# Three retention output units in seven-product form, with their operand's sums stored earlier, and a new order of the input projection

## The chip, the core and the metric

The kernel runs on one core of a Trainium2 chip. The core has a matrix engine (PE, with a separate row PEld for its weight loads), a vector engine (DVE), a scalar engine (ACT), a general engine (POOL) and a queue engine (SP). Each engine takes its instructions strictly in the order in which they were built, and waits on semaphores of the others. In this kernel SP issues nearly all transfers between HBM and on-chip memory; POOL issues a few.

The metric is the device time of one execution in microseconds (us). Smaller is better.

## What is computed

One layer of a gated hybrid encoder on 1024 positions with 1024 channels, all in float32. Cut to what matters here:

```python
h = rms_norm(x, norm1_w)
q, k, v, g_ret, x_lru, y_lru, gate_ret, gate_lru = split(h @ w_in)
o = head_group_norm(chunkwise_retention(rotary(q), rotary(k), v), ret_gn_w)
y_a = (o * silu(g_ret)) @ w_ret_o              # retention output
hl = rg_lru(causal_depthwise_conv(x_lru))
y_b = (hl * gelu(y_lru)) @ w_lru_o             # recurrent output
mix = sigmoid(gate_ret + b0) * y_a + sigmoid(gate_lru + b1) * y_b
x = x + mix @ w_out
x = x + (gelu(conv(h2 @ w_up_gate)) * (h2 @ w_up_val)) @ w_dn,  h2 = rms_norm(x)
return rms_norm(x)
```

## The kernel before

**Precision.** A float32 operand is split into two fast-format parts, `hi` (an ACT copy, line 167) and `lo` (a DVE subtraction, line 168), in the function `split`. A float32 product is three matrix instructions: hi·hi, hi·lo and lo·hi (`PASSES`).

**Units.** All large products are cut into units of 256 output channels, 1024 input channels and 1024 positions, a 2×2 by 2×2 block product. A unit has one of two forms.

- The standard form (`mm_std`, line 329): eight block products, each 4 column tiles × 3 passes = 12 matrix instructions of 128×512, so 96 in all. Its weights need four splits, and its results go from PSUM straight to the unit's own last step.
- The seven-product form (`mm_fast`, line 359, Strassen's scheme as Winograd arranged it): seven block products, 84 matrix instructions. Its weights need four sums (lines 245, 248, 254, 261) and seven splits. Three of its intermediate results are copied out of PSUM by ACT (line 374) and added by DVE (line 385). It also needs four sums of the moving operand, `T1` to `T4`, besides the four blocks `B11` to `B22`. Each of these names stands for four tiles of 128×512.

**Stages.** The stages follow each other on PE: the input projection (28 units), retention output (4 units, `w_ro`), recurrent output (4 units, `w_lo`), the output projection (line 1009), the up projection (24 units), and the down projection (12 units). The first two stages and the third form one list of jobs, `jobs`; the order of the input projection is written by hand in the string `SEQ`. A letter `g` is a merge-gate unit, `y` a gelu branch unit, `x` a recurrent branch unit followed by its recurrent block (`lru_block`), `h0` to `h3` are the three units of a retention head followed by its attention work (`rotary_head`, `retention_head`, `ret_out`). Before, `SEQ` ends in `... y3 x3`, so the last unit is a recurrent one and its block runs beside the retention output.

**Side work.** What follows a unit is a Python generator, and it is dealt out in small steps between the block products: `advance` for the recurrent and retention work, `build` for the splits of the next stage's operand (`operand`, `tsets`), as long as at least 20 of the `NU` = 78 buffers of 128×512 are free. `need` forces a split out when a product wants it. A scheduler then orders the instructions of each engine by these priorities.

**Retention output.** `ret_out` multiplies the normalised head by its gate and stores the result in HBM as `og_d` (line 837). When the last but one unit of the projection is done, `og_start` appends a builder that reads `og_d` back (line 867) and splits the 16 tiles of `B11` to `B22`. All four units have standard form (`FAST_RO = 0`), so no `T` sums are made. The three last recurrent output units have seven-product form (`FAST_LO = 3`); their operand `u` is read from `u_d` at line 867 too. `u_start` starts that builder when the third retention output unit is done, after draining the recurrent blocks.

Of the kernel before, what the change touches and what calls it, by code (L numbers as in the profile page):

```python
# [11 lines left out]
F32 = mybir.dt.float32  # L12
# [5 lines left out]
P = 128  # L18
D = 1024
T = 1024  # L20
KT = 8
TH = 512
# [64 lines left out]
class Units:  # L87
# [11 lines left out]
    def get(self, dt=F32):  # L99
        i = self.q.popleft()  # L100
        self.count += 1
        t = self.pool.tile(self.shape, dt, tag=f"{self.name}{i}", name=f"{self.name}{i}_{self.count}")
        self.at[id(t)] = (i, t)
        return t

    def put(self, *tiles):
        for t in tiles:
            self.q.append(self.at.pop(id(t))[0])


PASSES = ((0, 0), (0, 1), (1, 0))
NU = 78
NW = 22
NBLK = 7
AHEAD = 6
# [1 line left out]
RATE = 1.0  # L117
BRATE = 3.0
RESERVE = 20
FAST_RO = 0  # L120
RO_T = 9
FAST_LO = 3
GQ = False
SEQ = "g g y0 g y1 h0 h1 h2 h3 x0 g g x1 g y2 g x2 g y3 x3"
STD_L = 2


# [1 line left out]
def tile_trunk_layer(ctx, tc, x, positions, params, consts, normf, w_in, w_ro, w_lo,  # L129
# [18 lines left out]
    ident = cst[:, C_ID:C_ID + P]  # L148

    og_d = pdr.tile([KT, P, T], F32, tag="og", name="og_d")  # L150
    u_d = pdr.tile([KT, P, T], F32, tag="u", name="u_d")
    y_d = pdr.tile([KT, P, T], F32, tag="y", name="y_d")
    sg_d = pdr.tile([2, KT, P, T], F32, tag="sg", name="sg_d")
# [10 lines left out]
    def split(src, get=get):  # L164

        hi, lo = get(F32R), get(F32R)
        S.copy(hi, src)  # L167
        V.tensor_sub(lo, src, hi.bitcast(F32))  # L168
        return hi, lo
# [141 lines left out]
    def drain():  # L311
        while back:
            advance(1e9)
# [126 lines left out]
    def pair_src(w, i):  # L440
        return lambda m, kh: w[i, 2 * m + kh]
# [59 lines left out]
    def reads(fetch, keys, ahead):  # L501

        keys, got = deque(keys), deque()
        while keys or got:
            while keys and len(got) <= ahead:
                got.append(fetch(*keys.popleft()))
            yield got.popleft()

    def tsets(op, fetch, ahead=2):
        tiles = reads(fetch, [(n, j) for j in range(4) for n in ("B11", "B12", "B21", "B22")], ahead)  # L510
        for j in range(4):
            b11, b12, b21, b22 = (next(tiles) for _ in range(4))
            t1, t2 = get(), get()
            V.tensor_sub(t1, b12, b11)
            op["T1", j] = split(t1)
            yield 1.2
            V.tensor_sub(t2, b22, t1)
            op["T2", j] = split(t2)
            yield 1.2
            V.tensor_sub(b12, b22, b12)  # L520
            op["T3", j] = split(b12)
            V.tensor_sub(t2, b21, t2)  # L522
            op["T4", j] = split(t2)
            put(t1, t2, b11, b12, b21, b22)
            yield 2.4
# [242 lines left out]
    def retention_head(hd, qk, vv):  # L768
        cur = 0
        mask = cst[:, C_MASK + 128 * hd:C_MASK + 128 * hd + 128]  # L770
        for h in range(2):
# [52 lines left out]
                yield 0.3  # L824
            put(kd[h], vt[h, 0], vt[h, 1], qk[0, h], qk[1, h])

    def ret_out(hd, gg):
        for h in range(2):
            for m in range(2):
                ps = psa.get()  # L830
                for b in range(4):
                    c0 = 256 * (b % 2) + 128 * m
                    PE.transpose(ps[:, 128 * b:128 * b + 128], ob[h, b // 2][:, c0:c0 + 128], ident)
                g = gg[m, h]
                V.scalar_tensor_tensor(g, ps, pc("ret_gn_w", 2 * hd + m), g, ALU.mult, ALU.mult)
                psa.put(ps)
                ST.dma_start(og_d[2 * hd + m, :, TH * h:TH * h + TH], g)
                put(g)
                yield 0.8
            put(ob[h, 0], ob[h, 1])  # L840
        if hd == HEADS - 1:
            put(*rot.values())
# [10 lines left out]
    def operand(op, fetch, sums=True):  # L853

        keys = [(n, j) for n in ("B11", "B21", "B12", "B22") for j in range(4)]
        for key, t in zip(keys, reads(fetch, keys, 3)):
            op[key] = split(t)
            put(t)
            yield 0.6
        if sums:  # L860
            yield from tsets(op, fetch)

    def from_dram(src):
        def fetch(n, j):
            t = get()
            h = int(n[2]) - 1
            SY.dma_start(t, src[4 * (int(n[1]) - 1) + j, :, TH * h:TH * h + TH])
            return t
        return fetch
# [18 lines left out]
    def emit_ret_o(n):  # L888
        def emit(m, h, ps, unit):
            ch = 2 * n + m  # L890
            t = ojobs[n].take(m, h)
            V.tensor_mul(t, ps, t)
            ST.dma_start(t1_d[ch, :, TH * h:TH * h + TH], t)
            put(t)
            if unit is not None:
                put(unit)
        return emit
# [46 lines left out]
    jobs[-1].last = True  # L944
    def og_start(post=jobs[-2].post):
        builders.append(operand(og, from_dram(og_d), False))
        return post() if post else None

    jobs[-2].post = og_start

    def og_sums():
        drain()
        if FAST_RO:
            builders.append(tsets(og, from_dram(og_d)))

    def u_start():
        drain()
# [1 line left out]

    ojobs = []  # L960
    for n in range(4):
        ojobs.append(Job(pair_src(w_ro, n), og, emit_ret_o(n), {2: u_start, RO_T: og_sums}.get(n),
                        fast=n >= 4 - FAST_RO, last=n == 3, drop12=n == 3 - FAST_RO, fetch=from_sg(0, n)))
    for n in range(4):
        ojobs.append(Job(pair_src(w_lo, n), u, emit_lru_o(n), fast=n >= 4 - FAST_LO, last=n == 3,
# [239 lines left out]
```

## Time and profile before

| what | us |
|---|---|
| median of three runs | 1688.11 |
| the three runs | 1681.28, 1688.11, 1688.87 |
| the profiled execution, its own time | 1682.55 |
| its span, first to last instruction | 1680.8 |

| engine | busy us | share of the span | instructions |
|---|---|---|---|
| PE (matrix products) | 1629.0 | 97% | 7284 |
| PEld (weight loads) | 1335.7 | 79% | 7284 |
| DVE | 1252.8 | 75% | 2295 |
| ACT | 888.4 | 53% | 1467 |
| POOL | 40.6 | 2% | 60 |

A row of a group reads: line of the source, engine, operation, written tile `<-` read tiles, shape, count, then busy time in us and the mean duration of one in ns, then the idle time of that engine just ahead of the group and who ended it. A row of the timeline reads: start in us, length in us, engine, line, operation, count, and in brackets the idle time of the engine ahead of it with its releaser. A row of the windows reads: the stretch, its length, then busy time and count of instructions for PE, PEld, DVE, ACT and POOL, the granted PE clock, the busy share of the transfer engines, and GB/s. `SPq` is a transfer issued from SP. Instructions overlap within an engine, so a start-to-start distance is shorter than a duration. The line numbers are those of the kernel before.

On the time axis of the trace the input projection runs from 20 us to about 665 us. The retention output starts at 657 us, and its last result is gated by DVE at 779 us (line 892). The recurrent output lasts to 855 us, the output projection (line 1009) to 949 us, the up projection to about 1440 us, and the down projection to the end. Neighbours overlap.

### The profile page before, as it was taken

Reading aid. Unit: us, or ns where it says so; the run is one execution under the profiler, and the core shown is the slowest. Engines: PE = TensorE matmul, PEld = TensorE weight load, DVE = VectorE, ACT = ScalarE, POOL = GpSimd, SP = SyncE. Lnnn points to the kernel's source line nnn. Section 1 sums busy time; section 2 is a strip of 40 time slices with the busy share of each in tenths; the row PEclk is TensorE's granted clock in tenths of the full one; section 3 lists DMA queues with packets and bytes.
Section 4 is the critical chain, followed back from the end, with each engine's and each line's share of the span. In section 5 each row is a group of like instructions: output and inputs, shape, how many; then the busy total and the mean of one; then the engine's idle time right before and its main releaser. Section 6 shows DMA issues by size and latency. Waiting matters only on the chain.

```text
span 1680.8 us, 21200 instructions
## 1 busy us (share of the span) xinstructions
PE 1629.0 (97%) x7284; PEld 1335.7 (79%) x7284; DVE 1252.8 (75%) x2295; ACT 888.4 (53%) x1467; POOL 40.6 (2%) x60
## 2 busy tenths in 40 slices
PE   6999999999999999999999999999999999899997
PEld 5888888878887887887778788888888887678776
DVE  7986676676777878858972797677776777878886
ACT  6663434445478978853440564444444455453554
POOL 0010000000000000000000000000000000000000
PEclk9999999999999999999999999999999999999999
DMA  5253132231333437647553123222222347687762
GB/s 192 89 147 97 32 100 67 72 88 44 94 120 99 146 103 256 199 161 252 187 185 110 65 76 99 84 82 82 82 88 82 88 120 231 219 263 238 258 205 75
DMA packets 118220, 221.78 MB, mean 132 GB/s; under 512 B 13792, under 2 KB 13920, under 8 KB 118112
## 3 DMA queue, kind: packets, MB, share of 16 engines
q1 hardware_dynamic: 113888, 206.79, 39.0%
q0 software_dynamic: 4224, 13.64, 2.7%
q8 instruction: 57, 0.93, 0.2%
q14 instruction: 51, 0.42, 0.1%
HBM read 160.60 MB, written 54.53 MB: 128 GB/s over the span
## 4 chain that ended last, share of the span: by engine, by line
PE 68%; issue 15%; DMA 6%; DVE 6%; ACT 3%; POOL 1%; SPq 1%; POOLq 0%; DVEq 0%; ACTq 0%
PE g L359 49%; PE g L329 8%; PE g L1009 4%; PE a L690 2%; DVE w L168 1%; DVE u L168 1%; DMA x_d<-u 1%; POOL ff_d L1047 1%; DMA w<-w_in 1%; PE a L797 1%; PE a L799 1%; PE a L808 1%; DMA u_d<-u 1%; PE a L483 1%; DMA u<-w_dn 1%
## 5 line engine op out<-in xcount | busy, mean ns | idle before, releaser
L359 PE MATMUL g<-u,w 128*128 128x512 f32 x5124 | 1203.3, 393 | 20.9 <-ACT u L374 9.2
L359 PEld LDWEIGHTS g<-u,w 128*128 128x128 f32 x5124 | 957.8, 188 | 225.4 <-ACT u L374 14.8
L167 ACT CAST w<-w 128x512 fp32r<-128x512 f32 x471 | 291.2, 622 | 386.0 <-PE g L359 304.0
L168 DVE TENSOR_TENSOR w<-w,w 128x512 fp32r<-128x512 f32 x471 | 322.5, 686 | 95.8 <-ACT w L167 87.1
L329 PE MATMUL g<-u,w 128*128 128x512 f32 x1056 | 248.3, 391 | 0.0
L329 PEld LDWEIGHTS g<-u,w 128*128 128x128 f32 x1056 | 196.8, 188 | 41.6 <-ACT u L487 1.1
L167 ACT CAST u<-u 128x512 fp32r<-128x512 f32 x232 | 139.1, 620 | 142.3 <-DVE u L522 18.4
L168 DVE TENSOR_TENSOR u<-u,u 128x512 fp32r<-128x512 f32 x232 | 154.4, 686 | 37.2 <-ACT u L167 27.8
L385 DVE TENSOR_TENSOR u<-g,u 128x512 f32<-128x512 f32 x183 | 125.8, 688 | 68.9 <-PE g L359 50.5
L374 ACT COPY u<-g 128x512 f32<-128x512 f32 x183 | 106.2, 580 | 67.1 <-PE g L359 66.1
L1009 PE MATMUL g<-u,u 128*128 128x512 f32 x384 | 89.7, 392 | 1.4 <-ACT u L167 1.4
L1009 PEld LDWEIGHTS g<-u,u 128*128 128x128 f32 x384 | 71.5, 188 | 16.5 <-ACT u L167 1.9
L1042 DVE SCALAR_TENSOR_TENSOR u<-u,par,u 128x511 f32<-128x511 f32 x96 | 71.7, 747 | 6.8 <-ACT u L1039 6.0
L1047 POOL DMA_DIRECT2D ff_d<-u x48 | 36.1, 751 | 1291.6 <-DVE u L1046 1283.2
L245 DVE TENSOR_TENSOR w<-w,w 128x512 f32<-128x512 f32 x61 | 42.1, 689 | 21.9 <-DMA w<-w_up 11.8
L690 PE MATMUL a<-u,u 128*128 128x512 f32 x192 | 47.8, 392 | 3.3 <-ACT u L167 3.3
L1039 ACT ACTIVATE u<-u,par 128x512 f32<-128x512 f32 x48 | 39.2, 816 | 18.0 <-DVE u L385 14.7
L1011 DVE TENSOR_TENSOR u<-g,u 128x512 f32<-128x512 f32 x16 | 11.0, 691 | 47.2 <-PE g L1009 47.2
L690 PEld LDWEIGHTS a<-u,u 128*128 128x128 f32 x192 | 35.5, 188 | 12.7 <-ACT u L167 4.6
L248 DVE TENSOR_TENSOR w<-w,w 128x512 f32<-128x512 f32 x61 | 42.0, 688 | 1.0
L261 DVE TENSOR_TENSOR w<-w,w 128x512 f32<-128x512 f32 x61 | 41.9, 686 | 0.5
L254 DVE TENSOR_TENSOR w<-w,w 128x512 f32<-128x512 f32 x61 | 41.8, 686 | 0.4
(160 smaller groups left out, 1078.7 us busy)
## 6 DMA issues: line engine op xcount, KB each, us to landing
w<-w_in SPq DMA_DIRECT2D x112, 256.0 KB, 2.7
w<-w_up SPq DMA_DIRECT2D x96, 256.0 KB, 2.7
u<-w_dn SPq DMA_DIRECT2D x96, 256.0 KB, 4.1
u<-x_d SPq DMA_DIRECT2D x56, 256.0 KB, 4.5
x_d<-u SPq DMA_DIRECT2D x48, 256.0 KB, 2.7
ff_d<-u POOLq DMA_DIRECT2D x48, 256.0 KB, 2.7
w<-ff_d SPq DMA_DIRECT2D x48, 256.0 KB, 3.6
u<-x SPq DMA_DIRECT2D x32, 256.0 KB, 5.1
```

The costliest lines, as they stand in the source:

```text
L167: S.copy(hi, src)
L168: V.tensor_sub(lo, src, hi.bitcast(F32))
L245: V.tensor_add(s1, a21, a22)
L248: V.tensor_sub(s1, s1, a11)
L329: PE.matmul(ps[h], w[a][:, c], o[b], start=n == 0, stop=n == 23)
L359: PE.matmul(bank, w[a][:, c], need(op, (bn, j))[b], start=first and n == 0, stop=n == 11, skip_group_check=True)
L374: S.copy(u, bank)
L385: V.tensor_add(u, bank, u)
L690: PE.matmul(ps, wg[g][a][:, cs], xs[k][b], start=q == 0, stop=q == 5)
L1009: PE.matmul(ps, o[a][:, 128 * t:128 * t + 128], wo[k][b], start=n == 0, stop=n == 23)
L1042: V.scalar_tensor_tensor(c[:, s:], src[:, :TH - s], w, c[:, s:], ALU.mult, ALU.add)
L1047: G.dma_start(ff_d[g, 4 * h:4 * h + 4, kh, :, kk, :].rearrange("t p c -> p t c"), c.rearrange("p (t c) -> p t c", t=4))
```

## The change

1. The retention output takes the seven-product form in its last three units (`FAST_RO = 3`). The first stays standard.
2. The sums `T1` to `T4` of that operand are not built from re-read blocks by `tsets`. A new generator, `out_sums`, makes them inside `ret_out` of the heads 2 and 3, from the blocks of heads 0 and 1, read back from `og_d`, and those just finished. They are stored in a new HBM tensor `to_d`, 16 tiles of 128×512. Another new generator, `kept_sums`, reads them back and splits them, after the 16 blocks.
3. `SEQ` changes: the heads start one unit earlier, the recurrent units come earlier, and the projection ends in `x3 g g`.
4. There are 81 instead of 78 buffers (`NU`). The room comes from halving the ring for transfers that POOL describes, `dynamic_dma_scratch_size=8192`.
5. The unused `og_sums` and `RO_T` go away.

```diff
-NU = 78
+NU = 81
-FAST_RO = 0
-RO_T = 9
+FAST_RO = 3
-SEQ = "g g y0 g y1 h0 h1 h2 h3 x0 g g x1 g y2 g x2 g y3 x3"
+SEQ = "g g y0 y1 h0 h1 h2 h3 x0 y2 g x1 y3 g x2 g g x3 g g"
+    to_d = pdr.tile([4, 4, P, TH], F32, tag="to", name="to_d")
+    def out_sums(j, b21, b22):
+        b11, b12 = get(), get()
+        for h, b in ((0, b11), (1, b12)):
+            SY.dma_start(b, og_d[j, :, TH * h:TH * h + TH])
+        yield 1.0
+        V.tensor_sub(b11, b12, b11)
+        ST.dma_start(to_d[0, j], b11)
+        yield 0.6
+        V.tensor_sub(b12, b22, b12)
+        ST.dma_start(to_d[2, j], b12)
+        put(b12)
+        yield 0.6
+        V.tensor_sub(b11, b22, b11)
+        ST.dma_start(to_d[1, j], b11)
+        put(b22)
+        yield 0.6
+        V.tensor_sub(b21, b21, b11)
+        ST.dma_start(to_d[3, j], b21)
+        put(b21, b11)
+        yield 0.6
     def ret_out(hd, gg):
...
                 ST.dma_start(og_d[2 * hd + m, :, TH * h:TH * h + TH], g)
-                put(g)
                 yield 0.8
+                if hd < 2:
+                    put(g)
+                elif h == 1:
+                    yield from out_sums(2 * hd - 4 + m, gg[m, 0], g)
+    def kept_sums(op, src):
+        def fetch(n, j):
+            t = get()
+            SY.dma_start(t, src[int(n[1]) - 1, j])
+            return t
+        keys = [(f"T{i}", j) for i in (1, 2, 3, 4) for j in range(4)]
+        for key, t in zip(keys, reads(fetch, keys, 3)):
+            op[key] = split(t)
+            put(t)
+            yield 0.6
     def og_start(post=jobs[-2].post):
         builders.append(operand(og, from_dram(og_d), False))
+        builders.append(kept_sums(og, to_d))
         return post() if post else None
-    def og_sums():
-        drain()
-        if FAST_RO:
-            builders.append(tsets(og, from_dram(og_d)))
-        ojobs.append(Job(pair_src(w_ro, n), og, emit_ret_o(n), {2: u_start, RO_T: og_sums}.get(n),
+        ojobs.append(Job(pair_src(w_ro, n), og, emit_ret_o(n), {2: u_start}.get(n),
-    nc = bacc.Bacc("TRN2", target_bir_lowering=False, num_devices=1)
+    nc = bacc.Bacc("TRN2", target_bir_lowering=False, num_devices=1, dynamic_dma_scratch_size=8192)
```

## The prediction

> **What bounds the kernel now.** I read the page's busy shares first, then the groups by line, then PE's own timeline for its gaps, and last the busy times by stretch.
>
> ```profile
> PE 1629.0 (97%) x7284; PEld 1335.7 (79%) x7284; DVE 1252.8 (75%) x2295; ACT 888.4 (53%) x1467; POOL 40.6 (2%) x60
> ```
>
> PE is nearly always busy, but its durations overlap, so the pitch says more. In PE's timeline two long runs without a gap follow each other:
>
> ```profile
> 54.69 14.44 PE L329 MATMUL g<-u,w 128*128 128x512 f32 x63
> 68.97 21.24 PE L359 MATMUL g<-u,w 128*128 128x512 f32 x93
> ```
>
> 63 standard-form instructions take 68.97 - 54.69 = 14.28 us, which is 0.2267 us each. Those of the seven-product form have the same pitch: (21.24 - 0.39) / 92 = 0.2266, with 0.39 us for the length of the last. A removed matrix instruction is worth 0.2267 us if nothing else holds PE. DVE and ACT have pitches of their own, from runs of equal operations in the timeline:
>
> ```profile
> 1403.47 2.19 ACT L167 CAST u<-u 128x512 fp32r<-128x512 f32 x4 [0.32 <-DMA u<-w_dn]
> 1422.49 2.50 DVE L168 TENSOR_TENSOR u<-u,u 128x512 fp32r<-128x512 f32 x4 [0.77 <-ACT u L167]
> ...
> ```
>
> ```profile
> L168 DVE TENSOR_TENSOR w<-w,w 128x512 fp32r<-128x512 f32 x471 | 322.5, 686 | 95.8 <-ACT w L167 87.1 <-PE g L329 3.6 <-PE g L359 3.5
> L167 ACT CAST w<-w 128x512 fp32r<-128x512 f32 x471 | 291.2, 622 | 386.0 <-PE g L359 304.0 <-issue 30.7 <-DVE w L248 18.8
> L385 DVE TENSOR_TENSOR u<-g,u 128x512 f32<-128x512 f32 x183 | 125.8, 688 | 68.9 <-PE g L359 50.5 <-ACT u L374 17.7
> L374 ACT COPY u<-g 128x512 f32<-128x512 f32 x183 | 106.2, 580 | 67.1 <-PE g L359 66.1 <-DVE u L728 0.6 <-ACT u L848 0.3
> L723 DVE TENSOR_TENSOR_SCAN u<-u,st,u 128x512 f32<-128x512 f32 x8 | 10.2, 1280 | 0.1
> ```
>
> A DVE operation of 128x512 lasts 0.686 us, but four take 2.50, so the next one starts after (2.50 - 0.686) / 3 = 0.60 us. For the ACT copy it is (2.19 - 0.622) / 3 = 0.52 us. These pitches, not the durations, price added work.
>
> PE does stop at the two handovers that the change touches. The first is from the input projection to the retention output:
>
> ```profile
> 656.88 1.29 PE L329 MATMUL g<-u,w 128*128 128x512 f32 x5
> 659.02 5.05 PE L359 MATMUL g<-u,w 128*128 128x512 f32 x21 [0.84 <-ACT u L374]
> 664.78 0.72 PE L690 MATMUL a<-u,u 128*128 128x512 f32 x2 [0.71 <-ACT u L167]
> ...
> 667.20 3.35 PE L329 MATMUL g<-u,w 128*128 128x512 f32 x14
> 671.75 0.73 PE L690 MATMUL a<-u,u 128*128 128x512 f32 x2 [1.21 <-ACT u L167]
> ```
>
> The loss at each is start to start less count times pitch: 2.14 - 1.13 = 1.0, 5.76 - 4.76 = 1.0, 4.55 - 3.17 = 1.4, together 3.4 us. Two of the three waits are for the gates of the last recurrent block (line 690). The second handover is into the recurrent output and on to the output projection:
>
> ```profile
> 791.70 4.92 PE L359 MATMUL g<-u,w 128*128 128x512 f32 x21
> 798.93 3.01 PE L359 MATMUL g<-u,w 128*128 128x512 f32 x12 [2.31 <-ACT u L374]
> 803.27 44.78 PE L359 MATMUL g<-u,w 128*128 128x512 f32 x195 [1.32 <-ACT u L167]
> 849.97 5.75 PE L359 MATMUL g<-u,w 128*128 128x512 f32 x24 [1.93 <-ACT u L374]
> 855.56 9.29 PE L1009 MATMUL g<-u,u 128*128 128x512 f32 x40
> 866.29 3.93 PE L1009 MATMUL g<-u,u 128*128 128x512 f32 x16 [1.43 <-ACT u L167]
> ```
>
> In the same way: 2.5 + 1.6 + 2.5 + 1.7 = 8.2 us. The side engines there, by stretch:
>
> ```profile
> 560.00:680.00 120.00, 117.24 (x511) 94.93 (x510) 98.89 (x169) 97.62 (x145) 0.00 (x0) 1.00 0.55 175
> 680.00:780.00 100.00, 100.00 (x443) 82.81 (x442) 70.93 (x115) 61.79 (x84) 0.00 (x0) 1.00 0.62 202
> 780.00:870.00 90.00, 83.01 (x361) 66.92 (x360) 81.00 (x132) 43.90 (x77) 0.00 (x0) 1.00 0.63 203
> ```
>
> DVE is at 82%, 71% and 90%; where it reaches 90%, PE loses most.
>
> **The change, part by part.** *Removed products.* Three units go from 96 to 84 matrix instructions: 36 × 0.2267 = 8.2 us off PE. The built order of the changed kernel confirms it: line 359 gains 252 and line 329 loses 288.
>
> *Added side work.* The built order adds 62 DVE operations of 128x512: per unit 3 weight splits, 4 weight sums and 3 additions like line 385 (30 for three units), 16 splits of the kept sums, 16 sums in `out_sums`. At 0.60 us that is 37 us. ACT gains 25 copies of 0.52 us and 9 like line 374 of about 0.48 us, 17 us, and loses five table loads.
>
> ```profile
> L693 ACT ACT_TABLE_LOAD x11 | 14.1, 1283 | 0.2
> ```
>
> Those give back 5 × 1.28 = 6.4 us. ACT stays far from full.
>
> *`out_sums`* lies in the stage of the last heads, whose last head looks like this:
>
> ```profile
> 395.00:445.00 50.00, 49.96 (x241) 40.90 (x240) 33.33 (x84) 25.55 (x45) 0.00 (x0) 1.00 0.21 64
> ```
>
> DVE has 16.7 us free in 50, and the sums of one head need 8 × 0.60 = 4.8 us. PE's products cover them. Queued behind a late sum would be the group-norm scaling (line 823) that the transposes of line 833 wait for, which cost PE this in the whole trace:
>
> ```profile
> L833 PEld LDWEIGHTS a<-cst,u x64: 137/140/145, 208.4 to 444.2; 128*128 128x128 f32 x64
> ...
>   DVE u L823: 2.5, 4
> ```
>
> I put +0.5 us there, with 0 and 2.5 (the same again) as ends.
>
> *Transfers.* SP gets 40 more of 256 KB: 16 stores to `to_d`, 8 re-reads of `og_d`, 16 reads of `to_d`. Storing `og_d` and reading it are the nearest rows:
>
> ```profile
> L837 SPq DMA_DIRECT2D og_d<-u x16: 326/327/532, 211.0 to 446.0; - x16
> ...
> DMA to landing us min/median/max: 2.0/2.3/3.4
> ```
>
> ```profile
> L867 SPq DMA_DIRECT2D u<-og_d x16: 319/320/453, 627.4 to 662.6; - x16
> ...
> DMA to landing us min/median/max: 2.6/3.8/6.7
> ```
>
> An issue takes SP 0.33 us, 13 us in all, of which 16 reads (5 us) pass through the first handover. In the built order the first of these reads stands some 37 us of PE work ahead of the first product with a `T` tile, the last some 20 us ahead of its own. So they are hidden behind the standard unit, and I count 0. If each of the 16 came late by its share of a landing, 3.8 / 4, PE would pay 15 us; that is a rival below. The smaller ring concerns POOL's 48 issues alone:
>
> ```profile
> POOL ff_d L1047 <- DVE u L1046: 1283.2, 47, 867.7
> ```
>
> POOL waits nearly always and nothing else is queued on it. A delay of one landing would stay hidden, since the stored tiles are read a stage later. I count 0.
>
> *The new wait.* Two gate units now cover the last recurrent block, so its line 690 waits (2.4 us) should go. But the 32 splits of the retention operand compete for DVE with that block. In the built order, from the addition (line 385) that waits for one product of the last gate but one, up to the split that the first retention unit's fourth column tile waits for, DVE has 31 operations: 29 of about 0.60 us and two scans of about 1.2 us, 19.8 us. PE has 68 matrix instructions in the same stretch, 68 × 0.2267 = 15.4 us. The addition can't start before PE's product ends, so DVE can't work ahead, and PE must wait at least 4.4 us. Behind the late split stand on DVE the other splits of that operand and the convolution of the last recurrent block, which PE wants next; by the same count their need falls within 0.5 us of the delayed PE, so the wait isn't paid twice. A late `og_d` read ahead of it could add one landing, 3.8 us. I take 5.3 us (the 4.4, one ACT copy of 0.5 and its hand-offs) in place of the 3.4 us of before: +1.9 us, with +1.0 and +4.8 as ends.
>
> *Second handover.* The last retention unit is shorter and now itself needs DVE, while the recurrent operand is split. By the built order DVE has 61 us of work in the 60 us of PE work around this handover, where before it had 77 in the 80 around its own. Both are full, so I keep 8.2 us: 0, with -5 (the wait for the third unit's drain shrinks, since the block ends earlier) and +6 (the first new wait over again) as ends.
>
> *Buffers.* The three more may let down-projection splits start sooner; the built order moves only a few there. 0, ±2.
>
> Sum on the profiled execution's own time: 1682.55 - 8.2 + 0.5 + 1.9 + 0 = 1676.8, -0.34%. That execution is 5.6 us under the median of the runs (1688.11), whose scatter of 7.6 us is as large as the change. I add half of the 5.6, since a new median may fall at either end: 1680 us.
>
> A half-speed spell of PE would add to the new wait. After one idle stretch the trace has
>
> ```profile
> 1513.62 4.60 PE L359 MATMUL g<-u,w 128*128 128x512 f32 x12 [2.32 <-DVE u L385]
> ```
>
> Twelve instructions there take 4.60 - 0.39 = 4.2 us to the last start, where 11 × 0.2267 = 2.5 is usual: 1.7 us lost, while 2.31 us idle at 798.93 cost nothing of the kind. The Trainium skill ("TensorE: Matmul & The Clock Gate", Part 1) says that the clock halves after an idle window of about 3.4 us. By that rule, the new wait, which falls into parts below 3 us, would cost no spell, and the sum stays; by the row at 1513.62 it may, and the sum would be 1678.5. The trace doesn't agree with the rule's length here.
>
> **The rivals.** *Both handovers get smooth.* The last recurrent block ends before the retention output, so `u_start` has nothing to drain, `u` is read earlier, and with three more buffers the second handover keeps only 3 of its 8.2 us. For it: three of the four waits there are for copies and splits that are late, not for PSUM. Against: the DVE count above. 1676.8 - 5.2 = 1671.6, with the same half added 1674.5: faster, by 0.65% on the profiled execution's scale.
>
> *DVE becomes the bound* from 680 us to the end of the recurrent output. Before, it is busy 70.93 + 81.00 = 151.9 us in 190. If the 46 added operations outside `out_sums` (27.7 us) all fall there, it needs 179.6 us. If it can't be filled beyond the 90% of the last stretch, 179.6 / 0.90 = 199.6 us: 9.6 us longer than before, with the saved products hidden under it. 1682.55 + 9.6 = 1692, with the half 1695: slower. It decides from the point at which more than 19 of the 27.7 us fall behind 680 us (190 × 0.90 - 151.9 = 19.1). Against it: the 16 kept-sum splits are placed mostly before the first retention unit ends. A row that speaks for it:
>
> ```profile
> 640.00:660.00 20.00, 19.16 (x83) 15.15 (x82) 18.09 (x30) 17.80 (x32) 0.00 (x0) 1.00 0.87 282
> ```
>
> At 90% again, PE lost time.
>
> *The sums arrive late*, 15 us as above: 1676.8 + 15 = 1692, with the half 1695: slower. The transfer engines' 0.87 in that row speaks for it, the lead of 20 us and more against.
>
> **How the numbers follow.** A measurement of this kernel can tell about 0.5% from no change, 8.4 us. My forecast (-0.34%) gets 0.45 and lies within; the smooth handovers get 0.38, faster; DVE as the bound 0.13 and late sums 0.04, slower. So 0.38 faster, 0.45 within, 0.17 slower. The forecast's own range, with its terms' ends taken as independent (roots of the sums of squares: 5.5 down, 7.2 up), is 1674 to 1687. To hold 8 in 10 it has to reach into the faster case and close to the slower ones: 1669 to 1692.
>
> **What would show it.** Right: line 359 has 252 more instructions; PE's timeline at the first handover has a wait of 4 to 6 us before a line 329 instruction, released by DVE's line 168; the line 690 waits are gone; the second handover still loses some 8 us. Wrong: no wait for an operand split at the first handover (then DVE had worked ahead), DVE at 90% or more from 680 us on with many short PE gaps, PE waits for `to_d` reads, or a change in stages that the edit leaves alone.

## The result and the profile after

The changed kernel takes 1690.27 us (median of 16 runs, 1688.46 to 1698.17). The kernel before, run beside it, takes 1684.55 us (16 runs, 1680.89 to 1691.86). The ratio is 1.0034, with a 95% interval of 1.0022 to 1.0046: the change costs 0.34%, where a gain of 0.34% was forecast (1682.55 to 1676.8 us on the profiled execution's own time). The profiled execution takes 1690.67 us with a span of 1688.9 us; before it was 1682.55 and 1680.8.

To see where 8.1 us of span came from, PE's loss is counted: from every PE record of a trace the time from its start to the next start, less the usual time of its shape (0.2267 us for 512 columns), summed over a stretch. The last row is the part of that loss that falls on runs of four or more instructions at about half the usual pace.

| stretch, us | before | after |
|---|---|---|
| 0 to 560 | 11.6 | 8.8 |
| 560 to 720, first handover | 4.4 | 13.8 |
| 720 to 880, second handover | 8.3 | 17.3 |
| 880 to 1400 | 2.0 | 1.8 |
| 1400 to the end | 21.7 | 22.6 |
| whole | 47.9 | 64.3 |
| of it at half speed | 2.8 | 11.4 |

The books close: 36 products less are -8.2 us, 64.3 - 47.9 = +16.4 us, together +8.2. Both handovers take more than the products give. Line numbers of the kernel after are those of before up to line 826; behind it they are 22 to 38 higher, so the read of `og_d` and `u_d` is line 905 and the output projection line 1044. The groups by line of the kernel after show that the edit itself is as counted (line 359 has 252 more, line 329 288 fewer), and the busy times by stretch answer to those shown of before:

```profile
L359 PE MATMUL g<-u,w 128*128 128x512 f32 x5376 | 1269.6, 394 | 18.7 <-ACT u L374 14.3 <-ACT u L167 2.2 <-ACT u L1080 1.5
L329 PE MATMUL g<-u,w 128*128 128x512 f32 x768 | 187.4, 397 | 6.9 <-ACT u L167 4.2 <-DVE u L168 2.6
```

```profile
560.00:680.00 120.00, 112.90 (x475) 90.13 (x474) 92.89 (x153) 94.09 (x140) 0.00 (x0) 0.96 0.48 149
680.00:780.00 100.00, 95.30 (x401) 76.33 (x400) 84.53 (x141) 69.13 (x107) 0.00 (x0) 0.97 0.70 226
780.00:870.00 90.00, 85.16 (x362) 68.20 (x362) 80.00 (x132) 43.68 (x76) 0.00 (x0) 0.98 0.72 235
```

DVE does not reach 90% in any of the three, and in the first it is busy for less time than before (98.89). PE's granted clock, 1.00 in all three before, is now below 1. PE's timeline of the kernel after, first at the handover into the retention output, then at those into the recurrent output and the output projection:

```profile
664.51 2.57 PE L329 MATMUL g<-u,w 128*128 128x512 f32 x10 [0.38 <-DVE u L168]
670.22 1.22 PE L329 MATMUL g<-u,w 128*128 128x512 f32 x2 [3.14 <-ACT u L167]
673.47 5.06 PE L329 MATMUL g<-u,w 128*128 128x512 f32 x11 [2.02 <-DVE u L168]
...
765.81 0.73 PE L329 MATMUL g<-u,w 128*128 128x512 f32 x2 [0.17 <-DVE u L168]
769.67 8.28 PE L359 MATMUL g<-u,w 128*128 128x512 f32 x24 [3.13 <-ACT u L374]
...
856.38 1.16 PE L1044 MATMUL g<-u,u 128*128 128x512 f32 x3 [3.07 <-ACT u L167]
857.34 7.10 PE L359 MATMUL g<-u,w 128*128 128x512 f32 x24
```

Each long wait is followed by slow work: 24 instructions last 8.28 us, where (24 - 1) × 0.2267 + 0.39 = 5.6 us is usual. The windows of the same trace show the granted clock there (the column before the last two):

```profile
672.00:680.00 8.00, 6.53 (x16) 5.16 (x17) 5.93 (x10) 3.17 (x7) 0.00 (x0) 0.53 0.58 167
...
770.00:776.00 6.00, 6.00 (x17) 4.70 (x17) 4.04 (x7) 2.43 (x5) 0.00 (x0) 0.58 0.61 207
...
857.00:861.00 4.00, 4.00 (x12) 3.17 (x11) 4.00 (x8) 2.80 (x5) 0.00 (x0) 0.57 0.67 220
```

What PE waits for is found by going one engine further back each time. ACT, DVE and SP of the kernel after at the first handover:

```profile
665.45 1.14 ACT L167 CAST u<-u 128x512 fp32r<-128x512 f32 x2 [2.10 <-DMA u<-og_d]
...
669.57 0.60 ACT L167 CAST u<-u 128x512 fp32r<-128x512 f32 x1
```

```profile
666.10 0.69 DVE L168 TENSOR_TENSOR u<-u,u 128x512 fp32r<-128x512 f32 x1 [1.64 <-ACT u L167]
...
668.45 0.69 DVE L728 TENSOR_TENSOR u<-u,u 128x512 f32<-128x512 f32 x1
...
672.73 1.89 DVE L168 TENSOR_TENSOR u<-u,u 128x512 fp32r<-128x512 f32 x3
```

```profile
660.30 0.32 SPq L905 DMA_DIRECT2D u<-og_d  x1
...
669.35 0.40 SPq L729 DMA_DIRECT2D u_d<-u  x1
```

The read of `og_d` issued at 660.30 lands 5 us later, and ACT stands 2.10 us waiting for it. DVE runs dry behind ACT (1.64 us), so a recurrent block's product on line 728 comes only at 668.45. In the built order this is the last product of the block of `x2`, the last but one; the block of `x3` has just begun. The `hi` part of the fourth `B11` tile goes into a buffer that this product reads, so its cast starts at 669.57 and PE at 670.22. The `lo` part goes into the buffer that the product writes, which is free when its store to `u_d`, issued at 669.35, has landed; that split starts at 672.73, and PE at 673.47. The tile itself was among the first four read. So the operand waits for buffers that the block of `x2` still holds. DVE is idle for 1.64 us just ahead of PE's first wait and for 0.45 us in it. At the second handover of the kernel after:

```profile
764.41 0.62 ACT L167 CAST u<-u 128x512 fp32r<-128x512 f32 x1 [0.87 <-DMA u_d<-u]
...
768.52 0.62 ACT L167 CAST u<-u 128x512 fp32r<-128x512 f32 x1 [2.96 <-DMA u<-u_d]
769.04 0.58 ACT L374 COPY u<-g 128x512 f32<-128x512 f32 x1
...
855.08 1.25 ACT L167 CAST u<-u 128x512 fp32r<-128x512 f32 x2 [1.72 <-DMA u<-w_out]
```

```profile
730.73 0.32 SPq L905 DMA_DIRECT2D u<-u_d  x1
...
758.89 0.42 SPq L729 DMA_DIRECT2D u_d<-u  x1
...
762.70 0.32 SPq L729 DMA_DIRECT2D u_d<-u  x1
764.45 0.80 SPq L905 DMA_DIRECT2D u<-u_d  x2
```

Here it is the block of `x3`. Its last result but one is stored from 758.89; the store lands at 764.39, the read back starts at 764.45 and lands at 768.50, and the split starts at 768.52. (The store of the very last result, at 762.70, is read back from 767.25.) The copy of line 374, which frees the PSUM bank that PE wants, stands behind that cast in ACT's queue. The store itself was late too: the product of line 728 that it stores had ended at 754.27, and the store stood 4.6 us in SP's queue behind reads that waited for buffers. The third long wait, at 856.38, ends with a cast that waited 1.72 us for a read of `w_out`; no run here follows it up. The first read of `u_d` starts at 730.73; in SP's timeline of the kernel before it is 36 us earlier:

```profile
694.65 0.32 SPq L867 DMA_DIRECT2D u<-u_d  x1
```

### The profile page after: what moved, and what is told of

Its sections match the earlier page's. It is cut to its first block, busy times and chain, and to the rows that moved or that the text cites. A ratio compares the mean times of both kernels' runs of the same rounds, so it can differ in the third digit from the quotient of the medians.

```text
span 1688.9 us, 21311 instructions
## 1 busy us (share of the span) xinstructions
PE 1633.4 (97%) x7248; PEld 1336.7 (79%) x7248; DVE 1286.7 (76%) x2357; ACT 898.8 (53%) x1496; POOL 40.7 (2%) x60
## 4 chain that ended last, share of the span: by engine, by line
PE 66%; issue 15%; DVE 8%; DMA 6%; ACT 3%; POOL 1%; SPq 0%; POOLq 0%; DVEq 0%; ACTq 0%
PE g L359 49%; PE g L329 6%; PE g L1044 5%; PE a L690 2%; DVE w L168 2%; DMA u<-w_dn 2%; DVE u L168 1%; POOL ff_d L1082 1%; DMA w<-w_in 1%; PE a L797 1%; PE a L483 1%; PE a L799 1%; PE a L808 1%; ACT u L167 1%; DVE u L673 1%
## 5 line engine op out<-in xcount | busy, mean ns | idle before, releaser
L359 PEld LDWEIGHTS g<-u,w 128*128 128x128 f32 x5376 | 1011.2, 189 | 233.7 <-ACT u L374 19.4
L167 ACT CAST w<-w 128x512 fp32r<-128x512 f32 x480 | 296.7, 622 | 384.6 <-PE g L359 306.8
L168 DVE TENSOR_TENSOR w<-w,w 128x512 fp32r<-128x512 f32 x480 | 328.8, 686 | 88.4 <-ACT w L167 84.4
L167 ACT CAST u<-u 128x512 fp32r<-128x512 f32 x248 | 149.0, 620 | 143.7 <-DMA u<-w_dn 16.3
L168 DVE TENSOR_TENSOR u<-u,u 128x512 fp32r<-128x512 f32 x248 | 165.2, 687 | 38.3 <-ACT u L167 31.4
L385 DVE TENSOR_TENSOR u<-g,u 128x512 f32<-128x512 f32 x192 | 132.0, 687 | 69.0 <-PE g L359 55.1
L374 ACT COPY u<-g 128x512 f32<-128x512 f32 x192 | 111.7, 582 | 72.5 <-PE g L359 70.0
L1077 DVE SCALAR_TENSOR_TENSOR u<-u,par,u 128x511 f32<-128x511 f32 (+1 forms) x96 | 71.6, 747 | 6.1 <-ACT u L1074 5.4
L245 DVE TENSOR_TENSOR w<-w,w 128x512 f32<-128x512 f32 x64 | 44.1, 689 | 21.9 <-DMA w<-w_up 13.0
L1046 DVE TENSOR_TENSOR u<-g,u 128x512 f32<-128x512 f32 x16 | 10.9, 690 | 46.9 <-PE g L1044 46.9
L248 DVE TENSOR_TENSOR w<-w,w 128x512 f32<-128x512 f32 x64 | 44.0, 688 | 0.9
L261 DVE TENSOR_TENSOR w<-w,w 128x512 f32<-128x512 f32 x64 | 43.9, 686 | 0.5
L254 DVE TENSOR_TENSOR w<-w,w 128x512 f32<-128x512 f32 x64 | 43.8, 685 | 0.3
```

Source lines behind the costliest of these rows:

```text
L245: V.tensor_add(s1, a21, a22)
L248: V.tensor_sub(s1, s1, a11)
L359: PE.matmul(bank, w[a][:, c], need(op, (bn, j))[b], start=first and n == 0, stop=n == 11, skip_group_check=True)
L374: S.copy(u, bank)
L385: V.tensor_add(u, bank, u)
L1077: V.scalar_tensor_tensor(c[:, s:], src[:, :TH - s], w, c[:, s:], ALU.mult, ALU.add)
```

## The experiments

Theory D is the prediction's: the seven-product units give DVE too much to do. Theory L: the reads of `og_d` are late because they stand behind gate stores on SP. Theory M: the reads and splits are late because of buffers, handed on in the order of the program while a recurrent block still holds them, and because the last block ends late. Theory C: the clock halves because PE stood idle. All ratios are to the kernel before, run beside; losses are PE's, in us, from one profile each. A profile is a single execution, up to 3.7 us away from the median of its kernel's runs, so small differences of losses mean little.

| run | ratio, 95% interval | 560–720 | 720–880 | half speed |
|---|---|---|---|---|
| changed kernel | 1.0034, 1.0022–1.0046 | 13.8 | 17.3 | 11.4 |
| e1 order and buffers | 0.9999, 0.9983–1.0014 | 9.5 | 7.0 | 6.7 |
| e2 old order | 1.0062, 1.0037–1.0086 | 8.3 | 22.8 | 6.4 |
| e3 buffers | 0.9969, 0.9952–0.9986 | 4.8 | 11.1 | 3.6 |
| e4 gate stores on POOL | 1.0075, 1.0053–1.0096 | 15.4 | 19.4 | 8.2 |
| e5 block first | 0.9986, 0.9974–0.9998 | 9.5 | 14.4 | 5.5 |
| e6 standard unit last | 1.0035, 1.0021–1.0049 | 14.8 | 16.8 | 9.5 |
| e7 78 buffers | 1.0048, 1.0032–1.0065 | 15.3 | 18.9 | 10.1 |
| e8 blocks early | 1.0095, 1.0078–1.0111 | 18.5 | 17.9 | 8.9 |
| e9 `u` early | 1.0020, 1.0008–1.0032 | 14.6 | 16.0 | 5.2 |
| e10 extra products | 1.0056, 1.0038–1.0075 | 10.1 | 17.9 | 7.4 |
| e11 e5 and e9 | 0.9979, 0.9967–0.9991 | 9.2 | 9.5 | 3.6 |
| e12 e11, standard units | 0.9995, 0.9980–1.0010 | 12.6 | 6.0 | 6.9 |
| e13 before, mended | 0.9996, 0.9985–1.0007 | 5.0 | 11.1 | 3.6 |
| e14 e11, six reads ahead | 0.9950, 0.9935–0.9964 | 8.4 | 15.3 | 5.4 |
| e15 e11, reserve 14 | 0.9990, 0.9980–1.0000 | 7.3 | 18.1 | 5.2 |
| e16 e11, eight reads ahead | 0.9986, 0.9977–0.9996 | 9.9 | 15.0 | 4.2 |
| e17 changed, six reads ahead | 1.0026, 1.0015–1.0038 | 11.4 | 22.1 | 6.5 |
| e18 e3, six reads ahead | 0.9962, 0.9949–0.9974 | 4.7 | 12.9 | 5.6 |

**The change taken apart.** e1 is the kernel before with the new order and buffers, e3 with the buffers alone, e2 the changed kernel with the old order, e7 with the old number of buffers.

```diff
 # e1 and e3, on the kernel before; SEQ in e1 only
-NU = 78
+NU = 81
-SEQ = "g g y0 g y1 h0 h1 h2 h3 x0 g g x1 g y2 g x2 g y3 x3"
+SEQ = "g g y0 y1 h0 h1 h2 h3 x0 y2 g x1 y3 g x2 g g x3 g g"
-    nc = bacc.Bacc("TRN2", target_bir_lowering=False, num_devices=1)
+    nc = bacc.Bacc("TRN2", target_bir_lowering=False, num_devices=1, dynamic_dma_scratch_size=8192)
 # e2, on the changed kernel
-SEQ = "g g y0 y1 h0 h1 h2 h3 x0 y2 g x1 y3 g x2 g g x3 g g"
+SEQ = "g g y0 g y1 h0 h1 h2 h3 x0 g g x1 g y2 g x2 g y3 x3"
 # e7, on the changed kernel
-NU = 81
+NU = 78
```

> The kernel before with only the new order of the input projection and the 81 buffers with the smaller ring; all retention output units stay standard, no sums. Theory L (late reads: the last reads of og_d sit in SP's queue behind the stores of the two last gate units, which wait for ACT, and ACT waits for those reads): the stores are still there, so the first handover (640 to 700 us) still loses 5 to 9 us where before lost 4.5; no units are shortened, so 1.002 to 1.004 of before. Theory D (DVE has too many splits for the fast operand): with 16 splits instead of 32 the wait is gone, first handover under 3 us, ratio 0.998 to 1.000.

> The changed kernel with the old order of the input projection (it ends in y3 x3). Theory L: the last unit's results are not stored at once, so SP's queue is free for the og_d reads and the wait for them shrinks; the gates of the last recurrent block come back (2 to 3 us). First handover 4 to 7 us instead of 10.3, ratio to before 0.997 to 1.001. Theory D: the last recurrent block and all 32 splits now meet on DVE in the standard unit, so the first handover is worse than in the changed kernel, over 12 us, ratio 1.004 to 1.008.

> The kernel before with 81 buffers and the smaller ring alone. If the buffers or the ring cost something by themselves (the wait of 3.6 us that the changed kernel has at 1420 us, start of the down projection), the ratio is 1.001 to 1.003 and that wait is there. If not: 0.998 to 1.000.

> The changed kernel with 78 buffers again. Theory M: three buffers fewer make the reads later still; the two handovers together lose 3 to 8 us more than in the changed kernel, ratio 1.005 to 1.009. Theory D: DVE's work is the same, ratio 1.002 to 1.004 like the changed kernel.

The buffers alone gain 0.31%, more than was expected. With them the new order gives it back (e3 to e1, +0.30%, though the two intervals overlap a little), and the seven-product units with their stored sums cost another 0.35% (e1 to the changed kernel); with the old order they cost 0.93% (e3 to e2). So the units, which save 8.2 us, cost time in either order. e1 loses 7.2 us from 640 to 700 us, as theory L had it, but its ratio is the one of theory D. e2's ratio lies in theory D's band, but its first handover is better, as theory L had it; what is worse is its second, which neither theory had, with one wait of 7.09 us there, for line 941, the product of the recurrent output with its merge gate. e7 falls at the border of both expectations (1.0048); its interval overlaps the changed kernel's, so it shows nothing about theory M.

**SP's queue.** e4 issues the stores of the last two gate units from POOL.

```diff
-            ST.dma_start(sg_d[which, 2 * n + m, :, TH * h:TH * h + TH], t)
+            (G if which + 2 * n >= 6 else ST).dma_start(sg_d[which, 2 * n + m, :, TH * h:TH * h + TH], t)
```

> The changed kernel with the eight stores of the last two gate units issued from POOL instead of SP. Theory L: the reads of og_d no longer stand behind those stores; the two waits of 3.1 and 2.0 us at the start of the retention output shrink to under 3 us together, the half-speed stretch after them goes, the first handover loses 4 to 6 us instead of 10.3; ratio to before 0.999 to 1.001. Theory D: DVE's work is the same, so the waits stay at 5 us, first handover 9 to 11 us, ratio 1.003.

The kernel got slower, the first handover kept its two waits (2.98 and 1.69 us), and the late read of `og_d` was issued at 660.22, against 660.30 in the changed kernel. Theory L fell for the first handover; that led to following the buffers in the built order, and to theory M.

**The recurrent blocks.** e5 builds what is left of them, from the end of the last recurrent unit on, at the high priority that the operand's splits have. e8 orders the recurrent units so that four gate units end the projection.

```diff
 # e5; state["x3"] is set when the last recurrent unit is done
 ...
-            c = next(back[0], None)
+            with (hp() if state.get("x3") else nullcontext()):
+                c = next(back[0], None)
 # e8
-SEQ = "g g y0 y1 h0 h1 h2 h3 x0 y2 g x1 y3 g x2 g g x3 g g"
+SEQ = "g g y0 y1 h0 h1 h2 h3 x0 y2 x1 y3 g x2 g x3 g g g g"
```

> The changed kernel with the last recurrent block's instructions built at the same high priority as the operand splits. Theory M (buffers are handed on in program order, and the splits of the retention operand wait for buffers that the last recurrent block still holds; its last u_d stores are late too): the block lets go of its buffers sooner, the waits of 3.1 and 2.0 us at 667 to 673 us shrink to under 3 us together, the last u_d store comes well before 755 us; first handover 640 to 720 us loses 5 to 8 us instead of 11.6, ratio to before 0.998 to 1.001. Theory D (DVE has too much work in that stretch, whoever goes first): the sum of waits stays, others wait instead, ratio 1.002 to 1.006.

> The changed kernel with the recurrent units earlier, so that four gate units end the projection and the last recurrent block is done before the retention output starts. Theory M: no split waits for the block's buffers; first handover (640 to 720 us) 3 to 6 us instead of 11.6; the second, where the T tiles still hold buffers, 12 to 17 instead of 17.3; ratio 0.997 to 1.000. Theory D: DVE has less to do beside the retention output, so the first handover improves too, by about the same, but the projection before it loses PE time where the blocks crowd, over 3 us between 400 and 640 us.

e5 turns the loss of 0.34% into a gain of 0.14%. PE's timeline of e5 (its line numbers are one higher) has no wait before a line 330 instruction left at the first handover; one for the block's gates has come later:

```profile
662.51 5.83 PE L330 MATMUL g<-u,w 128*128 128x512 f32 x25
669.38 0.50 PE L691 MATMUL a<-u,u 128*128 128x512 f32 x1 [1.04 <-ACT u L167]
...
680.06 16.03 PE L330 MATMUL g<-u,w 128*128 128x512 f32 x70
...
703.54 1.22 PE L691 MATMUL a<-u,u 128*128 128x512 f32 x2 [3.37 <-ACT u L167]
```

The loss from 640 to 680 us is 1.5 us, where the changed kernel has 10.3; with the later wait counted in, from 640 to 720 us, it is 7.0 against 11.5. DVE's work is the same, as the first part of the two pages says, after and e5:

```profile
PE 1633.4 (97%) x7248; PEld 1336.7 (79%) x7248; DVE 1286.7 (76%) x2357; ACT 898.8 (53%) x1496; POOL 40.7 (2%) x60
```

```profile
PE 1624.3 (97%) x7248; PEld 1331.5 (79%) x7248; DVE 1286.4 (77%) x2357; ACT 892.7 (53%) x1493; POOL 40.6 (2%) x60
```

From 560 to 680 us DVE is even busier in e5 than in the changed kernel (96.91 us against 92.89), while PE loses 4.1 us there instead of 12.7:

```profile
560.00:680.00 120.00, 117.75 (x513) 94.85 (x512) 96.91 (x159) 99.41 (x149) 0.00 (x0) 1.00 0.49 153
```

So at the first handover the order of the work is the cause and not its amount, and theory D is refuted there. e5 changes the order of the engines' queues along with the time at which buffers come free; that the buffers are the link is read from the built order and the trace above, and no run changes them alone. e8 missed for theory M: the waits before line 329 instructions shrank to 0.5 and 1.1 us, but the four gates at the end moved the crowd forward, with a wait of 5.2 us at 642 us for a copy of line 374, and the kernel got slower. The loss between 400 and 640 us rose by 11 us, as theory D had it, though from 560 to 640 us DVE was no busier than in the changed kernel (62.24 us against 62.31).

**The second handover.** e6 makes the last retention unit standard and gives the `T` tiles back before it. e9 drains the recurrent block and starts the recurrent operand one unit earlier. e11 has e5 and e9.

```diff
 # e6; dropt is a new argument of Job
 ...
-fast=n >= 4 - FAST_RO, last=n == 3, drop12=n == 3 - FAST_RO, fetch=from_sg(0, n)))
+fast=n in (1, 2), last=n == 3, dropt=n == 2, fetch=from_sg(0, n)))
-            if jb.last:
+            if jb.last or jb.dropt and bn[0] == "T":
 # e9
-emit_ret_o(n), {2: u_start}.get(n),
+emit_ret_o(n), {1: u_start}.get(n),
```

> The changed kernel with the retention units in the order standard, fast, fast, standard; the T tiles are given back during the third. So 24 products instead of 36 are saved (5.4 us), and 32 buffers are free when the recurrent operand is due. Theory M (the T tiles hold the buffers that the recurrent operand needs): the first read of u_d comes 20 us or more earlier than 730.7, and 720 to 880 us loses 7 to 10 us instead of 17.3; ratio 0.998 to 1.000. Theory D (the seven-product units load DVE): two of them remain, so the loss falls by about a third at most, 12 to 17 us stay, ratio 1.002 to 1.005.

> The changed kernel with the recurrent block drained, and the builder of the recurrent operand started, one retention unit earlier. Theory M (the reads of u_d are late because they are put into the program late and their buffers are still held): the first read of u_d comes 10 us or more before 730.7, the wait of 3.1 us at 769.67 is gone, 720 to 880 us loses 8 to 13 us instead of 17.3, ratio 0.999 to 1.002. If the T tiles alone hold the buffers, so that an earlier start changes nothing: 15 to 18 us stay, ratio 1.002 to 1.005.

> The changed kernel with both: the last recurrent block at high priority, and the recurrent operand started one unit earlier. Theory M: the two work on different waits, so first handover (640 to 720 us) 7 us as with the first alone, second (720 to 880) 7 to 11 us instead of 14.4; ratio 0.994 to 0.998. Theory D: one's gain is the other's loss, ratio 0.998 to 1.002.

e6 missed: the wait at 769.67 is gone, but one of 2.85 us came at 805 us. That the `T` tiles hold the buffers of the recurrent operand is not borne out. e9 alone moves little: its first read of `u_d` starts at 732.87, since the block it depends on ends no sooner. With e5's priority as well (e11), the last store to `u_d` comes at 739.25 instead of 762.70, and the second handover's loss falls from 17.3 to 9.5 us. The store alone does not explain that: e5 has it at 742.84 and still loses 14.4 us, 3 of them at half speed, where e11 has no half-speed spell. The ratio of 0.9979 lies just within what theory M gave, but its interval reaches into the band of theory D. DVE is busier there, as the busy times of e11 show:

```profile
680.00:780.00 100.00, 94.24 (x403) 75.56 (x401) 90.55 (x153) 62.48 (x99) 0.00 (x0) 0.98 0.79 255
```

PE loses 11.1 us in that stretch, more than the 9.4 us that the changed kernel loses at 84.5%. So at the second handover the busy times do not speak against theory D. What does is the trace of the changed kernel, where ACT waits for a read ahead of the copy that PE wants, and the total, which falls by 0.55% with all of DVE's work still there. As the cause of most of the slowdown theory D is refuted; what part DVE has in the loss that remains at the second handover is open.

**The clock.** e10 puts 20 matrix instructions with zero weights ahead of the two products that wait at the first handover.

```diff
 # warm() issues products of the zero tile zr
 ...
+                        if here and n in (9, 10):
+                            warm(ps[h], op["B11", 0][0], 12 if n == 9 else 8)
                         PE.matmul(ps[h], w[a][:, c], o[b], start=n == 0, stop=n == 23)
```

> The changed kernel with 20 extra matrix instructions with zero weights in the first retention unit, 12 ahead of the product that waits 3.1 us and 8 ahead of the one that waits 2.0 us; they add zeros to an open bank. Theory C (PE runs at half speed for a while because it stood idle for some 3 us): both idle stretches shrink to under 1.5 us, the half-speed instructions after 673.5 us are gone, and the changed kernel gains 2 to 3 us there, ratio to before 1.001 to 1.003 with nothing else changed. Rival (the half speed comes from something other than the idle time, load or contention): the half-speed stretch stays, 12 instructions at 0.427 us, and the ratio is 1.003 to 1.005.

```profile
665.22 2.92 PE L320 MATMUL g<-u,zr 128*128 128x512 f32 x12
667.98 0.39 PE L339 MATMUL g<-u,w 128*128 128x512 f32 x1
670.85 0.80 PE L339 MATMUL g<-u,w 128*128 128x512 f32 x1 [2.48 <-ACT u L167]
671.44 3.09 PE L320 MATMUL g<-u,zr 128*128 128x512 f32 x8
674.37 3.81 PE L339 MATMUL g<-u,w 128*128 128x512 f32 x16
```

In PE's timeline of e10 (its line numbers are ten higher, and line 320 is the extra products) the first twelve ran at once and left 2.48 us idle, so the wait wasn't filled. The half-speed stretch then fell on the eight extra ones (3.09 us), and the real products behind them ran at the usual pitch (16 in 3.81). No time was gained, and the run does not decide for theory C. The traces together say more. A stop is measured here as in the table of losses, start to start less the usual time, which is about 0.16 us more than the idle time in the brackets of a timeline. In the 20 profiles, a stop of 1.5 to 2.0 us is followed by four or more half-speed instructions 3 times in 75; 2.0 to 2.5 us, 20 in 43; 2.5 to 3.0 us, 17 in 28; 3.0 to 3.5 us, 14 in 17; above, 25 in 25 (6 others had another wait right behind them).

**Do the units pay, once mended?** e12 is e11 with standard units and no sums, e13 the kernel before with 81 buffers and both mendings. e14 and e16 are e11 with more reads ahead, e17 and e18 the changed kernel and e3 with six; e15 is e11 with a smaller reserve.

```diff
 # e14, e17, e18: 5 for 3; e16: 7 for 3
-        for key, t in zip(keys, reads(fetch, keys, 3)):
+        for key, t in zip(keys, reads(fetch, keys, 5)):
 # e15
-RESERVE = 20
+RESERVE = 14
```

> The same new order, 81 buffers, block at high priority and earlier start of the recurrent operand as the run that had both, but all retention output units standard and no stored sums. Theory M (the seven-product units cost time only through late reads): with these mended, the 36 saved products show, so this kernel is 4 to 8 us slower than the one with both; ratio to before 0.998 to 1.003. If the units cost their side work anyway: this kernel is as fast or faster, ratio 0.993 to 0.998.

> The kernel before with 81 buffers, its last recurrent block at high priority and the recurrent operand started one unit earlier; old order, standard units. Theory M: 81 buffers alone gave 0.997; the second handover loses 3 to 5 us less than the 11.1 there, ratio 0.993 to 0.997. Theory D: the block's work moves ahead of splits that PE waits for sooner, ratio 0.997 to 1.001.

> The kernel with both mendings and six instead of four reads of an operand asked for ahead. Theory M in the form that the reads are asked for too late: the waits for og_d and u_d shrink, 560 to 880 us loses 14 to 17 us instead of 18.7, ratio 0.995 to 0.997. In the form that buffers are what is short: two more buffers bound by each builder, nothing gained, ratio 0.998 to 1.001.

> The kernel with both mendings and splits made ahead down to 14 free buffers instead of 20. If splits are late because the reserve holds them back: 560 to 880 us loses 13 to 17 us instead of 18.7, ratio 0.994 to 0.997. If the buffers themselves are short: others wait for theirs, ratio 0.998 to 1.002.

> The run with both mendings and six reads ahead, now with eight. If reads are still late: 560 to 880 us loses 18 to 22 us instead of 23.7, ratio 0.992 to 0.995. If the buffers run out: 24 us or more, ratio 0.995 to 1.000.

> The changed kernel with six reads of an operand asked for ahead instead of four, and nothing else. If the reads are late because they are asked for late: 560 to 880 us loses 20 to 26 us instead of 31.1, ratio 0.996 to 1.000. If they are late because the last recurrent block holds their buffers: 28 us or more, ratio 1.001 to 1.005.

> The kernel before with 81 buffers and six reads ahead; standard units, old order. If the gain of earlier reads is the same for both forms: 0.992 to 0.995, and the seven-product units pay nothing over it. If it is tied to the two operands that follow each other in the seven-product form: 0.996 to 0.999.

With equal mending the seven-product kernel (e11) is 0.16% ahead of the standard one (e12); the intervals overlap, so of the 8.2 us of saved products some 2.7 us show by the ratios, and none is certain. Unmended, the units cost 8.2 us of saved products and 5.9 us (0.35%) more; mended, they still cost 5.5 of the 8.2 us, and what that rest is no run tells. Six reads ahead gain clearly only together with both mendings: e17 stays at 1.0026, e18 is no better than e3 beyond the noise, and e14 comes to 0.9950, the lowest ratio of all, faster than both kernels (the intervals of e3 and e18 overlap its own). Eight reads (e16) or a smaller reserve (e15) gain nothing over e11. Where e14's gain lies is open: its own profile (17.8 us lost from 1400 us on against e11's 20.7, but more at the second handover) has a longer span than e11's, 1677.1 against 1675.4 us; but e14's profile is the slowest of its six runs and e11's the fastest of its twelve. e13 missed for theory M and lies in theory D's band: the gain of the buffers does not show in its runs (its interval just touches e3's), though its profile shows no new loss. e12 is 2.7 us slower than e11, by the ratios, where theory M had 4 to 8. e17 came as theory M had it for reads whose buffers a block holds. The intervals of e18 and e14 overlap, so for the best of both forms too a gain of the units is not shown.

## Why the prediction failed, step by step

The sum gave -5.8 us on the profiled execution's own time, and the execution came out 8.1 us longer. The 13.9 us between them are 7.5 at the first handover and 9.0 at the second, less 3.3 ahead of 560 us, and 0.7 behind 880 us. The measured 1690.27 us lies inside the stated range, near its slow end; the way was wrong.

*Removed products* (-8.2 us) were right. *Added side work* was about right: DVE's busy time grew by 1286.7 - 1252.8 = 33.9 us, where 37 were counted, and ACT's by 10.4 us, where 17 - 6.4 were. *`out_sums`*: the stretch up to 560 us lost 2.8 us less than before, and against e1, which has the same order, 0.7 us more; +0.5 was right. *Transfers*: ACT waited 3 times for reads of `to_d`, 2.1 us in all, and none of PE's long waits leads back to them, so the rival of the late sums did not come.

*The new wait* failed. "31 operations ... PE must wait at least 4.4 us" took DVE's work for the cause. A wait of 5.2 us in two parts did come, before line 329 instructions, so near to the 5.3 us of the sum by luck: it hangs on buffers of the block of `x2`, where the count has operations and no buffers, DVE ran dry just ahead of it, and e5 takes it away with DVE's work unchanged. The two gate units did cover the last block's own gates (the idle time ahead of line 690 went from 3.3 to 1.5 us in all); that a block runs beside the operand's splits, to which its buffers go, was not looked at. The stretch 560 to 720 us lost 9.4 us more, where +1.9 was counted; 2.6 us of the loss are a half-speed spell.

*The second handover* failed most: "I keep 8.2 us: 0". It lost 9.0 us more. Both sides of that sum were DVE's work against PE's. What set the wait at 769.67 (3.13 us and a spell of 2.2 us behind it) was when a late store to `u_d` landed and what stood behind its read in ACT's queue; the wait at 856.38 (3.07 us and a spell of 1.6 us) was for a read of `w_out`. Before, the first reads of `u_d` began 36 us earlier. e5 and e9 together bring the loss to 9.5 us, near the 8.3 of before; which link of the chain they mend is not separated.

*The half-speed spell* was left out of the sum. It was 2.8 us in the trace of before and is 11.4 us after: 8.6 us, about as much as the whole slowdown. Some 6.3 us of the 11.4 are part of the two losses above, and the rest lies behind 1400 us, where all of the 2.8 us of before lay. The row at 1513.62 was the one to go by, and even its 1.7 us price one spell, where the trace of after has six and that of before two. The Trainium skill ("TensorE: Matmul & The Clock Gate", Part 1) has a free-running window of about 3.4 us for the gate. In the count above every stop over 3.5 us halved the clock, as that length would have it, but so did 37 of 71 between 2.0 and 3.0 us, where the traces disagree.

*Buffers*, counted as 0 ± 2 us, gained 0.31% by themselves, about 5 us; *the order* cost about as much, by ratios whose intervals overlap a little. The rival with DVE as the bound gave 1692 and 1695 us, near the 1690.27 that came, but by DVE at 90% or more from 680 us on, which the windows do not show (84.5% and 88.9%).

## What to carry to other kernels

Where buffers are handed on in program order, a generator that runs behind its place in the program delays whoever gets its buffers next: follow the buffer numbers across a handover, not only the engines' work. On an engine that works strictly in order, a copy that frees a bank for the matrix engine should not stand behind a conversion of a tile that is still on its way, nor a store behind reads that wait for buffers. A wait of the matrix engine of 2 to 3 us cost nearly twice its length in this kernel when the clock halved after it, while stops under 2 us brought that only 3 times in 75; so one long wait was worse than several short ones of the same sum.

## What the runs showed of the hardware

In three windows behind long waits the granted clock was 0.53 to 0.58. Such a spell lasted 5 to 13 instructions of 0.427 us, with 1.0 to 2.6 us lost each time. What decides whether an idle time between 2 and 3 us brings one is open: in the kernel before, 2.31 us at 798.93 did not and 2.32 us at 1513.62 did.
